# A block-Strassen feed-forward on one Trainium2 core: the block sums of its weights, made by VectorE or by accumulating loads

## The chip, the core and the metric

One core of a Trainium2 chip runs the whole step. Its engines are TensorE (PE, matrix products; PEld is its weight load), VectorE (DVE), ScalarE (ACT), GpSimd (POOL) and SyncE (SP, which here only issues loads and stores). Each engine runs its own instructions strictly in their written order and waits at an instruction until what it reads or overwrites is ready. The metric is the device time of one execution in microseconds (us). Before the change it was 1875.71 us, the median of three runs (1874.99 to 1875.91).

## The reference, cut to what matters

The program is one inference step of a two-layer decoder trunk for 576 token columns (a prompt of 512 and eight samples of eight). Each layer has a mixer (recurrent in the first layer, a state-space scan in the second), a feed-forward part and a gated embedding part, each behind an RMS norm:

```
def _swiglu(x, w1, w3, w2):
    return (jax.nn.silu(x @ w1) * (x @ w3)) @ w2
...
        x = x + mix
        x = x + _swiglu(_rmsnorm(x, W['g_ffn'][i]), W['ffn_w1'][i], W['ffn_w3'][i], W['ffn_w2'][i])
        x = x + _ple(x, p[i], W['ple_up'][i], W['ple_gate'][i], W['g_ple'][i])
```

`w1` and `w3` are 1024 x 2816 and `w2` is 2816 x 1024, all float32. The change is within `x @ w1` and `x @ w3`, of both layers.

## The kernel before

**Arithmetic.** Every float32 operand is kept as two fp32r tiles, a rounded high part and the rest (`whi`, `wlo` for weights, L171 to L176: ScalarE copies into `whi`, then VectorE, in some places GpSimd, subtracts into `wlo`). A product is three matmuls: high with high, high with low, low with high. Activations lie feature by token, 128 features to a tile; the 576 columns are two halves of 288.

**The up products.** `ffn` (L1057 on) does `x @ w1` and `x @ w3` by Strassen's scheme in the variant of Winograd: the weights of a pair of 128-column groups, called a block here and `p` in the code, are four quarter tiles `w13[p, 0..3]` of 128 x 1024 float32 (512 KB), and a block takes seven products of 24 matmuls (L1112 to L1121) instead of eight. In the order of TensorE they are: quarter 1 (`mmy`), the sum `u` of quarters 2, 3 and 0 (`mmx`), the sum of quarters 2 and 3 (`mmz`), the sum of quarters 2 and 0 (`mmx`), quarter 0 of the next block (`head`, L1128), quarter 3 (`mmx`), and `u` with quarter 1 added (`mmz`). There are 11 blocks in a layer, done in three parts of 4, 4 and 3 blocks (`PARTS`); behind each part the eight down products with `w2` follow (L1174 to L1175, matmuls of L210).

**The sums before.** SP loads the four quarters a second time into tiles `a2`, `a3`, `a0`, `a1` (L1154, by way of L1110), one buffer each. VectorE makes the sums: `a22 += a21` (L1157; both by their Strassen names), `u = a22 + a11` (L1158), `a21 += a11` (L1163), and after the second product has split `u`, `u += a12` (L1173). Each sum is then split into `whi` and `wlo` by L174 and L175. Plain quarters pass through `raw` tiles with two buffers (L166 to L169).

**What sets the order.** The code is written in the order of the data; a scheduler that works on a timed model of the engines sets the order of each engine's instructions when the program is built, and places waits on semaphores. A load is issued by SP when its tile's last readers are done, and SP's loads too stand in one order.

**Ahead of each feed-forward.** In the first layer the last instructions of the mixer are its output products: TensorE's `mm` (L193) into two PSUM buffers, VectorE's residual add (L361), and GpSimd's `wlo` for them (L175). The products of the embedding part (`ple_up`, L193 with `xah`) follow, and fill TensorE while the norm is made: squares (L349, L350), their sum over features (`ssq`, L233), the inverse root on VectorE (L236 to L246), the broadcast `rbc` on TensorE (L252) and its copy `rb` (L255). Then VectorE makes the scaled input (L1092) and the operands of the seven products. In the second layer the residual adds are done by GpSimd (L359) from a scaled copy that VectorE makes (L358).

Of the kernel before, what the change touches and what calls it, by code (L numbers as in the profile page):

```python
# [12 lines left out]
F = mybir.dt.float32  # L13
# [4 lines left out]
OP = mybir.AluOpType  # L18

P = 128  # L20
D = 1024
KD = D // P
# [58 lines left out]
def trunk(ctx, tc, a, stop=None):  # L81
    nc = tc.nc
    V, S, G, PE = nc.vector, nc.scalar, nc.gpsimd, nc.tensor

    cp = ctx.enter_context(tc.tile_pool(name="const", bufs=1))
    wp = ctx.enter_context(tc.tile_pool(name="weights", bufs=2))
# [44 lines left out]
    def tmp(tag, bufs=2, w=T, dt=F):  # L131
        return tp.tile([P, w], dt, tag=tag, name=tag, bufs=bufs)

    def bank(name="s", tag="s"):
        return pq.tile([P, 512], F, tag=tag, name=name)
# [20 lines left out]
    def split_to(dst, src, scale=None):  # L156
        hi, lo = dst
        if scale is None:
            S.activation(hi, src, AF.Copy)
            V.tensor_tensor(lo, src, hi.bitcast(F), op=OP.subtract)  # L160
        else:
            S.activation(hi, src, AF.Copy, scale=scale)
            V.scalar_tensor_tensor(lo, src, scale, hi.bitcast(F), op0=OP.mult, op1=OP.subtract)  # L163
        return hi, lo
# [6 lines left out]
    def wsplit(raw, kt, pool, bufs, w=1024, eng=V):  # L171
        hi = pool.tile([P, w], R, tag="whi", name="whi", bufs=bufs)[:, :kt * P]
        lo = pool.tile([P, w], R, tag="wlo", name="wlo", bufs=bufs)[:, :kt * P]
        S.activation(hi, raw, AF.Copy)  # L174
        eng.tensor_tensor(lo, raw, hi.bitcast(F), op=OP.subtract)  # L175
        return hi, lo  # L176
# [6 lines left out]
    def wload(ap, kt, eng=V):  # L183
        return wsplit(wraw(ap, kt), kt, wp, 2, eng=eng)
# [874 lines left out]
    def ffn(i, ha):  # L1059
        w13, w2 = a["w13"][i], a["w2"][i]  # L1060
        with tc.tile_pool(name=f"ffn{i}", bufs=1) as hp:

            def hq():
                return [hp.tile([P, 4, T], R, tag="h" + t_, name="h" + t_, bufs=2) for t_ in "hl"]
# [12 lines left out]
            def operand(n, src, scale=None):  # L1077
                out = []
                for ks, hi, lo in keep(n):
                    split_to((hi, lo), src[:, ks[0]:ks[-1] + 1], scale)  # L1080
                    out += [(hi[:, j], lo[:, j]) for j in range(len(ks))]
                return out
# [18 lines left out]
            b1 = operand(3, d1)  # L1101
            b3 = operand(4, d3)
# [1 line left out]
            b4 = operand(5, d4)  # L1104
            b22 = operand(6, xg1[:, :, HF:])

            def wsum(tag, src=None):
                t = hp.tile([P, 1024], F, tag=tag, name=tag, bufs=1)
                if src is not None:
                    nc.sync.dma_start(t, src)  # L1110
                return t

            def prod(outs, wts, b, first):
                wh, wl = wts
                for n in range(2):
                    for k in range(4):
                        o = slice(n * SEQ + k * P, n * SEQ + (k + 1) * P)
                        h, l = b[k]
                        for t_, (w, v) in enumerate(((wh, h), (wh, l), (wl, h))):
                            PE.matmul(outs[n], w[:, o], v, start=(first and k == 0 and t_ == 0), stop=(k == 3 and t_ == 2),  # L1120
                                      skip_group_check=not first)  # L1121

            def copied(ps, tag):
                t = v2(tmp(tag, 2))
                S.activation(t, ps[:, :, :HF], AF.Copy)  # L1125
                return t

            def head(p):  # L1128
                ps = pm.tile([P, 2, 512], F, tag="mm", name="mmx")
                prod([ps[:, n, :HF] for n in range(2)], wload(w13[p, 0], KD), b11, True)  # L1130
                return ps, copied(ps, "t1")

            def block(s, outs, dst, sign):
                for n in range(2):
                    V.tensor_tensor(s[:, n], s[:, n], outs[n], op=OP.add)
                S.activation(s[:, 0], s[:, 0], AF.Silu, scale=sign)
                if sign > 0:
                    V.tensor_tensor(dst, s[:, 0], s[:, 1], op=OP.mult)
                else:
                    V.scalar_tensor_tensor(dst, s[:, 1], sign, s[:, 0], op0=OP.mult, op1=OP.mult)  # L1140

            for p0, p1 in PARTS:
                hs = []
                for p in range(p0, p1):
                    if p == p0:
                        ps, s1 = head(p)
                    if (p - p0) % 2 == 0:
                        hh, hl = hq()
                    o = 2 * ((p - p0) % 2)
                    xo = [ps[:, n, :HF] for n in range(2)]  # L1150
                    ys = [bank("mmy")[:, :HF] for _ in range(2)]
                    prod(ys, wload(w13[p, 1], KD), b21, True)
                    f1, f2 = tmp("rb", 2), tmp("t2", 2)
                    block(s1, ys, f1[:, :HF], 1.0)  # L1154
                    a21, a22, a11, a12 = (wsum(f"a{n}", w13[p, n]) for n in (2, 3, 0, 1))
                    u = wsum("u")
                    V.tensor_tensor(a22, a22, a21, op=OP.add)  # L1157
                    V.tensor_tensor(u, a22, a11, op=OP.add)  # L1158
                    prod(xo, wsplit(u, KD, wp, 2), b2, False)
                    s2 = copied(ps, "t2")  # L1160
                    zs = [bank("mmz", "o")[:, :HF] for _ in range(2)]
                    prod(zs, wsplit(a22, KD, wp, 2), b1, True)
                    V.tensor_tensor(a21, a21, a11, op=OP.add)  # L1163
                    prod(xo, wsplit(a21, KD, wp, 2), b3, False)
                    s3 = copied(ps, "t1")
                    block(s3, zs, f2[:, HF:], -1.0)
                    if p + 1 < p1:
                        nxt = head(p + 1)
                    prod(xo, wload(w13[p, 3], KD), b4, False)
                    S.activation(f2[:, :HF], xo[0], AF.Silu, scale=-1.0)  # L1170
                    V.scalar_tensor_tensor(f2[:, :HF], xo[1], -1.0, f2[:, :HF], op0=OP.mult, op1=OP.mult)
                    split_to((hh[:, o + 1], hl[:, o + 1]), f2)
                    V.tensor_tensor(u, u, a12, op=OP.add)  # L1173
                    prod(zs, wsplit(u, KD, wp, 2), b22, False)  # L1174
                    block(s2, zs, f1[:, HF:], 1.0)  # L1175
                    split_to((hh[:, o], hl[:, o]), f1)
                    hs += [(hh[:, o + 1], hl[:, o + 1]), (hh[:, o], hl[:, o])]
                    ps, s1 = nxt
                for m in range(KD):
                    add_out(m, gemm(w2[m][:, 2 * p0 * P:2 * p1 * P], hs, False))  # L1180
# [278 lines left out]
```

## Time and profile before

| What | Before |
|---|---|
| median of the runs | 1875.71 us |
| the profiled execution's own time | 1873.93 us |
| its span | 1872.2 us |
| TensorE busy | 1748.0 us, 93% |
| VectorE busy | 1343.1 us, 72% |
| ScalarE busy | 811.7 us, 43% |
| GpSimd busy | 415.1 us, 22% |
| second loads of the quarters | 88 of 512 KB |
| bytes moved | 193.74 MB, mean 103 GB/s |

The span runs from the first to the last instruction of the profiled execution; the execution's own time holds what lies around it as well. Engines run side by side, so that their busy times don't add up; for this kernel the question at each place is on what TensorE waits. In the views below, a wait stands as "[idle before <- what ended it]" behind an instruction. A busy TensorE shows in the count of its matmuls as well: at full clock some 77 of them start in 10 us. TensorE's granted clock is given as a share of full speed.

### The profile page before, as it was taken

Reading aid. Unit: us, or ns where it says so; the run is one execution under the profiler, and the core shown is the slowest. Engines: PE = TensorE matmul, PEld = TensorE weight load, DVE = VectorE, ACT = ScalarE, POOL = GpSimd, SP = SyncE. Lnnn points to the kernel's source line nnn. Section 1 sums busy time; section 2 is a strip of 40 time slices with the busy share of each in tenths; the row PEclk is TensorE's granted clock in tenths of the full one; section 3 lists DMA queues with packets and bytes.
Section 4 is the critical chain, followed back from the end, with each engine's and each line's share of the span. In section 5 each row is a group of like instructions: output and inputs, shape, how many; then the busy total and the mean of one; then the engine's idle time right before and its main releaser. Section 6 shows DMA issues by size and latency. Waiting matters only on the chain. (4 is left out here: it accounts for less than half of the span.)

```text
span 1872.2 us, 32247 instructions
## 1 busy us (share of the span) xinstructions
PE 1748.0 (93%) x13134; PEld 1693.6 (90%) x13134; DVE 1343.1 (72%) x2256; ACT 811.7 (43%) x1341; POOL 415.1 (22%) x393
## 2 busy tenths in 40 slices
PE   7899989899999999989998999998959999999994
PEld 7789979899999999989987999998959999999994
DVE  6877784886377375588996897988587637737556
ACT  6654442554254143444553444535444325415332
POOL 2433343000000000033445537455510000000002
PEclk9999999899999999989998999999979999999997
DMA  5111113244244242312231322223315424424221
GB/s 191 57 62 66 68 49 130 83 160 139 91 162 154 87 147 71 118 41 72 103 111 68 109 104 85 96 100 108 118 52 167 133 86 168 147 91 144 71 80 51
DMA packets 63124, 193.74 MB, mean 103 GB/s; under 512 B 7040, under 2 KB 12800, under 8 KB 62976
## 3 DMA queue, kind: packets, MB, share of 16 engines
q1 hardware_dynamic: 62400, 191.10, 29.8%
q8 instruction: 103, 1.69, 0.4%
q10 hardware_dynamic: 576, 0.59, 0.1%
q14 instruction: 45, 0.37, 0.1%
HBM read 177.10 MB, written 14.56 MB: 102 GB/s over the span
## 5 line engine op out<-in xcount | busy, mean ns | idle before, releaser
L174 ACT ACTIVATE whi<-wraw 128x1024 fp32r<-128x1024 f32 (+2 forms) x213 | 221.5, 1040 | 392.6 <-PE mm L210 175.3
L175 DVE TENSOR_TENSOR wlo<-wraw,whi 128x1024 fp32r<-128x1024 f32 (+1 forms) x187 | 230.4, 1232 | 73.8 <-ACT whi L174 73.0
L1220 POOL TENSOR_TENSOR ev<-ev,rb 128x288 f32<-128x288 f32 x18 | 18.1, 1034 | 952.7 <-ACT rb L255 952.7
L1120 PE MATMUL mmx<-bh,whi 128*128 128x288 f32 x704 | 211.9, 301 | 14.8 <-ACT t L1125 9.3
L1120 PE MATMUL mmx<-bh,wlo 128*128 128x288 f32 x704 | 210.6, 299 | 4.8 <-DVE wlo L175 4.7
L1120 PE MATMUL mmx<-bl,whi 128*128 128x288 f32 x704 | 210.6, 299 | 2.9 <-DVE bl L163 2.9
L193 PE MATMUL mm<-xah,whi 128*128 128x288 f32 x632 | 191.4, 303 | 3.7 <-DVE hz L264 1.7
L193 PE MATMUL mm<-xal,whi 128*128 128x288 f32 x632 | 190.2, 301 | 0.0
L193 PE MATMUL mm<-xah,wlo 128*128 128x288 f32 x632 | 189.4, 300 | 0.0
L361 DVE TENSOR_TENSOR x<-mm,x 128x288 f32<-128x288 f32 x128 | 52.4, 451 | 169.1 <-PE mm L210 159.1
L193 PE MATMUL mm<-xch,whi 128*128 128x288 f32 x536 | 161.4, 301 | 2.9 <-DVE x L361 2.9
L193 PE MATMUL mm<-xch,wlo 128*128 128x288 f32 x536 | 160.8, 300 | 0.0
L193 PE MATMUL mm<-xcl,whi 128*128 128x288 f32 x536 | 160.7, 300 | 0.0
L210 PE MATMUL mm<-hl,whi 128*128 128x288 f32 x704 | 152.0, 296 | 0.0
L210 PE MATMUL mm<-hh,whi 128*128 128x288 f32 x704 | 151.7, 296 | 0.0
L210 PE MATMUL mm<-hh,wlo 128*128 128x288 f32 x704 | 151.3, 296 | 0.0
L1120 PEld LDWEIGHTS mmx<-bh,whi 128*128 128x128 f32 x704 | 134.5, 191 | 16.9 <-ACT t L1125 10.7
L1120 PEld LDWEIGHTS mmx<-bh,wlo 128*128 128x128 f32 x704 | 135.2, 192 | 6.6 <-DVE wlo L175 6.5
L1120 PEld LDWEIGHTS mmx<-bl,whi 128*128 128x128 f32 x704 | 134.9, 192 | 3.1 <-DVE bl L163 3.1
L193 PEld LDWEIGHTS mm<-xah,whi 128*128 128x128 f32 x632 | 120.0, 190 | 7.8 <-ACT lt L497 2.1
L193 PEld LDWEIGHTS mm<-xal,whi 128*128 128x128 f32 x632 | 120.2, 190 | 2.4 <-issue 1.8
L193 PEld LDWEIGHTS mm<-xah,wlo 128*128 128x128 f32 x632 | 120.1, 190 | 1.6 <-issue 0.9
(495 smaller groups left out, 4927.4 us busy)
## 6 DMA issues: line engine op xcount, KB each, us to landing
wraw<-w SPq DMA_DIRECT2D x98, 512.0 KB, 3.4
a<-w SPq DMA_DIRECT2D x88, 512.0 KB, 3.3
wraw<-w_sin SPq DMA_DIRECT2D x40, 512.0 KB, 3.3
wraw<-w_ein SPq DMA_DIRECT2D x22, 512.0 KB, 3.3
wraw<-wg SPq DMA_DIRECT2D x16, 512.0 KB, 3.2
s<-ss SPq DMA_DIRECT2D x16, 512.0 KB, 3.5
sss<-s SPq DMA_DIRECT2D x16, 512.0 KB, 2.8
wraw<-w_sout SPq DMA_DIRECT2D x16, 512.0 KB, 3.6
```

Source lines behind the costliest of these rows:

```text
L174: S.activation(hi, raw, AF.Copy)
L175: eng.tensor_tensor(lo, raw, hi.bitcast(F), op=OP.subtract)
L193: PE.matmul(ps, w[:, cols], v, start=(k == 0 and i == 0), stop=(k == n - 1 and i == 2))
L210: PE.matmul(ps[:, s, :HF], w[:, j * P:(j + 1) * P], m[:, half(s)], start=(k == 0 and i == 0), stop=(k == n - 1 and i == 2))
L361: V.tensor_tensor(xh, src, xh, op=OP.add)
L1120: PE.matmul(outs[n], w[:, o], v, start=(first and k == 0 and t_ == 0), stop=(k == 3 and t_ == 2), skip_group_check=not first)
L1220: eng.tensor_tensor(v, v, r[:, half(s)], op=OP.mult)
```

## The change

SP now loads one quarter into each of three tiles, `u`, `sa` and `sb`, which have two buffers each, and GpSimd issues loads of the further quarters that add onto the tile as they land (`accum_op`): two onto `u` ahead of its first use, one onto `sa`, one onto `sb`, and one more onto `u` when its first split has been made. The four additions on VectorE are gone.

```diff
-            def wsum(tag, src=None):
-                t = hp.tile([P, 1024], F, tag=tag, name=tag, bufs=1)
-                if src is not None:
-                    nc.sync.dma_start(t, src)
+            def wsum(tag, p, *blocks):
+                t = hp.tile([P, 1024], F, tag=tag, name=tag, bufs=2)
+                nc.sync.dma_start(t, w13[p, blocks[0]])
+                for n in blocks[1:]:
+                    add_block(t, p, n)
                 return t
+
+            def add_block(t, p, n):
+                nc.gpsimd.dma_start(t, w13[p, n], accum_op=OP.add)
...
-                    a21, a22, a11, a12 = (wsum(f"a{n}", w13[p, n]) for n in (2, 3, 0, 1))
-                    u = wsum("u")
-                    V.tensor_tensor(a22, a22, a21, op=OP.add)
-                    V.tensor_tensor(u, a22, a11, op=OP.add)
+                    u, s1_, s3_ = wsum("u", p, 2, 3, 0), wsum("sa", p, 2, 3), wsum("sb", p, 0, 2)
                     prod(xo, wsplit(u, KD, wp, 2), b2, False)
...
-                    prod(zs, wsplit(a22, KD, wp, 2), b1, True)
-                    V.tensor_tensor(a21, a21, a11, op=OP.add)
-                    prod(xo, wsplit(a21, KD, wp, 2), b3, False)
+                    prod(zs, wsplit(s1_, KD, wp, 2), b1, True)
+                    prod(xo, wsplit(s3_, KD, wp, 2), b3, False)
...
-                    V.tensor_tensor(u, u, a12, op=OP.add)
+                    add_block(u, p, 1)
                     prod(zs, wsplit(u, KD, wp, 2), b22, False)
```

The order of the instructions changes in these places. On VectorE, within a block (the first layer's second one), the rows before were these; `wlo<-a` are splits of sums:

```order
L175 TENSOR_TENSOR wlo<-a_3935,whi 128x1024
L175 TENSOR_TENSOR wlo<-wraw,whi 128x1024
L1157 TENSOR_TENSOR a_4185<-a_4185,a_4183 128x1024
L1163 TENSOR_TENSOR a_4183<-a_4183,a_4187 128x1024
L175 TENSOR_TENSOR wlo<-wraw,whi 128x1024
L1135 TENSOR_TENSOR t_4035<-t_4035,mmz 128x288 x2
L175 TENSOR_TENSOR wlo<-u,whi 128x1024
```

and they are now, with `sb` in the place of the tile `a`:

```order
L175 TENSOR_TENSOR wlo<-sb,whi 128x1024
L175 TENSOR_TENSOR wlo<-wraw,whi 128x1024 x2
L1139 TENSOR_TENSOR t_4031<-t_4031,mmz 128x288 x2
L1144 SCALAR_TENSOR_TENSOR t_3928<-t_4031 128x288
L175 TENSOR_TENSOR wlo<-u,whi 128x1024
```

The two additions for the next block no longer stand ahead of the split of a plain quarter. On GpSimd, at the end of the first layer's mixer, the difference is this (`-` before, `+` now; `wlo` belongs to the mixer's output products):

```order
-L175 TENSOR_TENSOR wlo<-wraw,whi 128x1024 x3
+L175 TENSOR_TENSOR wlo<-wraw,whi 128x1024 x2
+L1115 DMA u<-w 128x1024
+L1115 DMA sa<-w 128x1024
+L1115 DMA sb<-w 128x1024
+L175 TENSOR_TENSOR wlo<-wraw,whi 128x1024
```

Three accumulating loads of the first block now stand ahead of the last `wlo`, and each waits for the plain load beneath it. On GpSimd at the end of the second layer's mixer the rows before were these, `x_75`, `x_76` and so on being the eight tiles of the residual:

```order
L175 TENSOR_TENSOR wlo<-wraw,whi 128x1024
L359 TENSOR_TENSOR x_75<-x_75,t_14369 128x288
L359 TENSOR_TENSOR x_75<-x_75,t_14372 128x288
L175 TENSOR_TENSOR wlo<-wraw,whi 128x1024
L359 TENSOR_TENSOR x_76<-x_76,t_14400 128x288
L359 TENSOR_TENSOR x_76<-x_76,t_14403 128x288
L359 TENSOR_TENSOR x_77<-x_77,t_14437 128x288
L359 TENSOR_TENSOR x_77<-x_77,t_14440 128x288
```

and they are now:

```order
L1115 DMA u<-w 128x1024
L1115 DMA sa<-w 128x1024
L1115 DMA sb<-w 128x1024
L359 TENSOR_TENSOR x_75<-x_75,t_14347 128x288
L359 TENSOR_TENSOR x_75<-x_75,t_14350 128x288
L1115 DMA u<-w 128x1024
L1115 DMA sa<-w 128x1024
L359 TENSOR_TENSOR x_76<-x_76,t_14378 128x288
L359 TENSOR_TENSOR x_76<-x_76,t_14381 128x288
L175 TENSOR_TENSOR wlo<-wraw,whi 128x1024
L1115 DMA sb<-w 128x1024
```

Two more loads of `u` follow among the adds of the tiles behind: eight in all, three ahead of the first add and five between the adds. On TensorE the order of the matmuls within the feed-forward is the same as before. Ahead of the first layer's, the broadcast of the norm (`rbc`) stood before among matmuls of `ple_up` like this (`mm_3422` and `mm_3437` are two of its products, of 12 matmuls each):

```order
L193 MATMUL mm_3422<-xah_3346,wlo_3419 128x288
L252 MATMUL rbc_3531<-cst_73,ry_3516 128x128 x4
L252 MATMUL rbc_3537<-cst_73,ry_3516 128x64
L193 MATMUL mm_3437<-xah_3333,whi_3418 128x288
L193 MATMUL mm_3437<-xal_3334,whi_3418 128x288
```

and stands now:

```order
L193 MATMUL mm_3437<-xal_3347,whi_3418 128x288
L193 MATMUL mm_3437<-xah_3346,wlo_3419 128x288
L252 MATMUL rbc_3531<-cst_73,ry_3516 128x128 x4
L252 MATMUL rbc_3537<-cst_73,ry_3516 128x64
L193 MATMUL mm_3452<-xah_3333,whi_3418 128x288
```

Twelve matmuls that came behind the broadcast now come ahead of it.

## Rows read from the trace of the kernel before

**Rows 1.** Stretches (up, down): busy PE, PEld, DVE, ACT, POOL; clock, DMA share, GB/s

```profile
388.00:454.00 66.00, 63.88 (x478) 63.41 (x478) 53.14 (x68) 32.52 (x47) 0.00 (x0) 1.00 0.46 160
600.00:657.00 57.00, 57.00 (x430) 57.00 (x429) 21.51 (x32) 12.23 (x15) 0.00 (x0) 1.00 0.29 93
```

**Rows 2.** PE's waits, 375 to 750 and 1400 to 1750: total us, times, longest

```profile
PE mmx L1120 <- ACT t L1125: 4.7, 3, 1.6
PE mmx L1120 <- DVE wlo L175: 1.1, 2, 0.6
...
PE mmx L1120 <- DVE wlo L175: 3.4, 3, 1.6
```

**Rows 3.** Timeline of DVE and PE, 1449 to 1460 us: start, us, what

```profile
1450.73 1.23 DVE L175 TENSOR_TENSOR wlo<-wraw,whi 128x1024 fp32r<-128x1024 f32 x1 [1.92 <-ACT whi L174]
1454.33 1.22 DVE L1157 TENSOR_TENSOR a<-a,a 128x1024 f32<-128x1024 f32 x1 [2.37 <-DMA a<-w]
1455.59 1.23 DVE L1163 TENSOR_TENSOR a<-a,a 128x1024 f32<-128x1024 f32 x1
1456.73 1.22 DVE L175 TENSOR_TENSOR wlo<-wraw,whi 128x1024 fp32r<-128x1024 f32 x1
...
1458.01 0.40 PE L1120 MATMUL mmx<-bh,wlo 128*128 128x288 f32 x1 [1.61 <-DVE wlo L175]
```

**Rows 4.** Two of the four sums over the run: ns minimum/median/maximum

```profile
L1157 DVE TENSOR_TENSOR a<-a,a x22: 1224/1226/3197, 323.9 to 1716.6; 128x1024 f32<-128x1024 f32 x22
...
L1173 DVE TENSOR_TENSOR u<-u,a x22: 1214/1218/1220, 371.2 to 1729.9; 128x1024 f32<-128x1024 f32 x22
```

**Rows 5.** Timeline of DVE, PE and POOL at the first layer's mixer end

```profile
323.59 2.39 POOL L175 TENSOR_TENSOR wlo<-wraw,whi 128x1024 fp32r<-128x1024 f32 x1 [4.60 <-ACT whi L174]
...
323.87 3.20 DVE L1157 TENSOR_TENSOR a<-a,a 128x1024 f32<-128x1024 f32 x1 [0.91 <-DMA a<-w]
...
327.85 0.40 PE L193 MATMUL mm<-xch,whi 128*128 128x288 f32 x1 [2.17 <-DVE x L361]
331.61 0.37 PE L193 MATMUL mm<-xch,whi 128*128 128x288 f32 x1 [0.32 <-DVE x L361]
```

**Rows 6.** Timeline of PE and DVE from the first layer's norm on

```profile
347.05 1.22 PE L252 MATMUL rbc<-cst,ry 128*128 128x128 f32 x10
...
348.89 5.92 DVE L1092 SCALAR_TENSOR_TENSOR hh<-x,par,rb 128x576 f32<-128x576 f32 x8 [1.03 <-ACT rb L255]
```

**Rows 7.** Second layer's mixer end: POOL's waits 1338 to 1372; timelines

```profile
POOL x L359 <- DVE t L358: 11.8, 5, 6.7
...
1343.94 1.56 POOL L359 TENSOR_TENSOR x<-x,t 128x288 f32<-128x288 f32 x2 [6.71 <-DVE t L358]
...
1366.67 2.52 POOL L359 TENSOR_TENSOR x<-x,t 128x288 f32<-128x288 f32 x2 [1.95 <-DVE t L358]
...
1339.18 1.23 DVE L1157 TENSOR_TENSOR a<-a,a 128x1024 f32<-128x1024 f32 x1
...
1343.41 0.81 DVE L358 TENSOR_TENSOR t<-mm,rb 128x288 f32<-128x288 f32 x2
...
1370.84 2.26 PE L233 MATMUL ssq<-cst,acc 128*128 128x1 f32 x10 [7.17 <-DVE acc L350]
```

**Rows 8.** SP's issue of the second loads: ns minimum/median/maximum

```profile
L1110 SPq DMA_DIRECT2D a<-w x88: 327/328/433, 316.1 to 1713.3; - x88
```

**Rows 9.** Loads issued 380 to 450, then 310 to 330: us to landing; slices

```profile
a<-w SPq DMA_DIRECT2D x12, 512.0 KB, 3.3
...
a<-w SPq DMA_DIRECT2D x4, 512.0 KB, 7.6
...
GB/s 33 188 406 385 37 0 106 401 401 139 0 0 101 217 373 400 236 205 279 197 238 238 320 320 369 377 401 426 418 434 361 246 164 98 188 377 352 49 57 33
```

**Rows 10.** Timelines of DVE and ACT: the two splits of one block's u

```profile
391.47 1.23 DVE L175 TENSOR_TENSOR wlo<-u,whi 128x1024 fp32r<-128x1024 f32 x1
...
406.22 1.06 ACT L174 ACTIVATE whi<-u 128x1024 fp32r<-128x1024 f32 x1 [1.60 <-PE mmx L1120]
```

## The prediction

> **What bounds the kernel now.** I read the busy times by stretch first, because the change lives in the up products alone. In a stretch of three whole blocks [rows 1] TensorE is busy for 63.88 of 66 us and VectorE for 53.14, at full clock; GpSimd does nothing. TensorE bounds these stretches, and VectorE's share of 81% costs only where TensorE has to wait for it. So the next view is what TensorE waits for there [rows 2]. In nearly all of the two feed-forward parts it waits for ScalarE's copies, three times 1.6 us in each layer (4.7 us and 4.7 us; the same row for both), which the change doesn't touch, and for VectorE's `wlo`: 1.1 us in the first layer and 3.4 us in the second, five waits in 22 blocks. The timeline of the longest [rows 3] shows how they come about. VectorE ends a split at about 1452, then stands 2.37 us at L1157, whose quarter hasn't landed; L1163 follows, and only then the split of the plain quarter that TensorE needs: it waits 1.61 us. A late load thus stops VectorE's whole queue. Last I read the two places ahead of the feed-forward parts [rows 5 to 7], where VectorE's sums and now GpSimd's loads stand among work that TensorE waits for.
>
> **What goes.** 88 additions on VectorE: four kinds, 22 each, of some 1.22 us [rows 4], together 88 x 1.22 = 107 us. Nearly all lie beside TensorE's matmuls and are worth nothing. On the path are:
>
> - The `wlo` waits, 1.1 + 3.4 = 4.5 us. Without L1157, no load can stop VectorE there, and the split comes right behind ScalarE's copy. I take all 4.5. The bound below is 2.5, if the waits only shrink: then ScalarE's spacing of its copies holds part of them.
> - First layer, end of the mixer: a sum took 3.20 us beside a GpSimd `wlo` of 2.39 us that ran at the same time [rows 5], against 1.22 us undisturbed; TensorE then waited 2.17 and 0.32 us for the residual adds behind it, 2.5 us. But the new order puts twelve matmuls ahead of the broadcast `rbc`. A matmul takes 63.88 us / 478 = 0.13 us [rows 1], so that is 1.6 us. `rbc` to L1092 is the path here: `rbc` runs at 347.05, L1092 starts at 348.89 and paces the start of the feed-forward [rows 6]. So 2.5 - 1.6 = 0.9 us is left of it.
> - Second layer, end of the mixer: the sums from 1339.18 on hold the first scaled copy until 1343.41 [rows 7]; without them it starts up to 4.2 us earlier, of which I count two sums, 2.4 us, as the norm must be broadcast first.
>
> **What comes.** 22 x 3 = 66 loads by SP for 88, and 22 x 5 = 110 accumulating loads that GpSimd issues.
>
> *The issue.* No row before shows a load that GpSimd issues. Below, SP's issue of the same shape takes 0.33 us [rows 8]; above, GpSimd's own pass over such a tile takes 2.39 us [rows 5]. Both rows are near in their own way, the first in kind of work, the second in engine, so I take the middle, 1.4 us. In the feed-forward itself GpSimd is empty, and five issues are 7 us of a block of 22 us: hidden. Ahead of the second layer's they are not. Three issues fall into a stretch of 6.71 us in which GpSimd waited for its first add [rows 7], 4.2 us: hidden, if the plain loads beneath have landed. Five stand between the adds: 5 x 1.4 = 7.0 us, against waits of 11.8 - 6.7 = 5.1 us among the later adds [rows 7]. So GpSimd ends its adds 1.9 us later, and the last add is on the path: TensorE waited 7.17 us for the norm's sum that hangs on it. Against the 2.4 us gained above, I book this place as 0; its bounds are 2.4 gained, if an issue costs 0.33 us, and 5 x 2.39 - 5.1 - 2.4 = 4.4 lost.
>
> Ahead of the first layer's part, three issues stand before the last `wlo` of the mixer, which started at 323.59 and was needed by about 331.6 [rows 5]. The loads under it took 7.6 us to land [rows 9], from 316.1 [rows 8], thus until about 324; the third one comes a load's transfer of 1.25 us (worked out below) behind. Then 1.4 us, then the `wlo` of 2.39 us: done at 329.0, when TensorE, without its 2.5 us of waits, wants it at 329.1. So nothing is lost at 1.4 us; at 2.39 us two or three microseconds are. Range of this place: 2.5 gained to 2 lost.
>
> *The transfer.* A block moved seven loads of 512 KB (0.524 MB) in 22 us; now it moves eleven, five of which read or write the tile as well. In slices with loads back to back the engines moved 401 to 434 GB/s [rows 9], so a plain load costs them 0.524 / 0.42 = 1.25 us. If an accumulating load costs r plain ones, a block wants (6 + 5r) x 1.25 us: 13.8 us at r = 1, 20.0 at r = 2, 26.3 at r = 3. No row sets the bound above. I take 1.5, near the plain load, the only row there is: 16.9 us, hidden in the 22.
>
> The row [rows 9] knows plain loads alone. The Trainium skill (Collectives: The Full Stack, "The bandwidth ceiling: the fold count and why AG ≠ RS ≠ AR") speaks against the change: an add in the DMA engines needs two source reads through one read ring, and there halved the throughput, 32.35 against 62.28 GB/s. By that r is about 2, and 20.0 of 22 us are in use; no run before shows it. The sum stays as it is, but the margin is 10%, and a later fall of it is likelier than by r = 1.
>
> *The waits.* SP's loads wait for buffers as before, with two of each. GpSimd's queue has one new danger: the third load onto `u` must come between the two splits of `u`. The first ends at 391.47 + 1.23 = 392.7, the second starts at 406.22 [rows 10]: 13.5 us for its issue, transfer and landing, where a plain load takes 3.3 us [rows 9]. Behind it in the queue stand the loads for the next blocks, which are wanted half a block later or more. Cover enough for a landing of 5 to 8 us.
>
> **The sum.** 4.5 + 0.9 + 0 = 5.4 us less. The profiled execution took 1873.93 us (its span of 1872.2 and 1.7 around it), so 1868.5; the median of the runs, 1875.71, lies 1.8 above it, so I predict 1870.3. With the bounds: at best 4.5 + 2.5 + 2.4 = 9.4 less, 1866; at worst 2.5 - 2 - 4.4, 3.9 more, 1879.6.
>
> **Rivals.**
>
> *A, slower: the accumulating loads are too dear for the engines.* Place: every block. It decides from (22 / 1.25 - 6) / 5 = 2.3 plain loads each. At r = 3.3 a block wants 28.1 us, 6.1 too many: 24.5 in a part of four blocks, 18.4 in one of three. The down products between (57 us at a share of 0.29 [rows 1]) let four of a block's five sums run ahead, 4 x 3.3 x 1.25 = 16.5 us. What stays is 4 x 8.0 + 2 x 1.9 = 36 us: 1875.7 + 36 - 5 = 1906. At r = 4 it is over 100 us. Milder and in the same mechanism: the third load onto `u` lands after 13.5 us, and every block waits; a microsecond each gives 1892. For it: nothing in the trace bounds r, and the margin at 2 is small. Against: the engines' mean share is 0.46 in the up stretches [rows 1].
>
> *B, no change: GpSimd's queue gives it back.* If an issue takes 2.39 us, the two mixer ends lose 2 + 4.4 = 6.4 us and the 4.5 are spent: 1875.7 + 1.9 = 1877.6. For it: GpSimd is the slowest engine for everything else; against: SP's issue takes a seventh of that [rows 8].
>
> *C, no change: another wait stands behind the one removed.* TensorE's waits for `wlo` end with ScalarE's copies: if these are half of it, and the moved `rbc` eats the first layer's gain, 2.3 us remain: 1873.4. For it: 1.92 us of VectorE's idle time ahead of a split is put down to ScalarE [rows 3]. Against: that split wasn't waited for.
>
> **Chances.** Forecast 0.48, A 0.27, B 0.13, C 0.12. What a measurement can tell here from no change is 0.2%, 3.7 us. Of the forecast some 0.04 is below that. So faster 0.44, the same 0.04 + 0.13 + 0.12 = 0.29, slower 0.27. The range goes from 1865 to 1900: it takes in the forecast, B and C, and of A the milder half; what is left out is some 0.15 above and 0.02 below. The forecast's own range is 1866 to 1880, B and C being within it.
>
> **What would show it.** Right: VectorE's busy time in the run down by some 107 us and no wait of TensorE on `wlo` in the blocks but at their start; the six waits for ScalarE of 1.6 us unchanged; GpSimd's issues below 2 us; a DMA share in the up stretches between 0.6 and 0.9. The first layer's L1092 starts about 1 us earlier than 348.89, the second layer's sum of squares within 2 us of 1370.84. Wrong: TensorE waits on the split of `u`, `sa` or `sb`, which in turn waits on a load; then A holds, and the landing time of these loads gives r. If TensorE's waits ahead of the feed-forward parts grow while the blocks run clean, it is B.

## The result, and the profile after

The changed kernel takes 1906.11 us in the median of four runs (1901.38 to 1907.46) against 1875.35 us before (1874.83 to 1875.91): the ratio is 1.0159 with a 95% interval of 1.0141 to 1.0178. The forecast was 1870.3 with a range of 1865 to 1900: the time moved the other way, and it lies 6 us past the top of the range.

I read the page first. These are its busy line and its lines on the DMA queues (queue, packets, MB, and the time that their packets took as a share of 16 engines over the span of 1903.7 us):

```profile
PE 1760.1 (92%) x13134; PEld 1706.1 (90%) x13134; DVE 1249.4 (66%) x2168; ACT 814.0 (43%) x1341; POOL 510.2 (27%) x503
...
q1 hardware_dynamic: 59232, 179.56, 27.0%
q0 software_dynamic: 15840, 57.68, 16.3%
```

VectorE fell from 1343.1 to 1249.4 us: 93.7 us, of the 107 that 88 times 1.22 us make, since rows that follow each other at once overlap by about 0.1 us (in [rows 3], 1455.59 + 1.23 against 1456.73). GpSimd's own queue, q0, now carries the 110 added loads. Its share gives their price: 16.3% of 1903.7 us are 310 us, over 110 loads 2.82 us of all engines for each. The plain loads of q1 take 27.0% for 179.56 MB, which is 1.50 us for 512 KB.

The two stretches of [rows 1], now three blocks and a down part (columns as there):

```profile
388.00:454.00 66.00, 66.00 (x499) 66.00 (x497) 41.38 (x57) 33.97 (x48) 11.13 (x13) 1.00 0.91 231
600.00:657.00 57.00, 50.36 (x361) 50.12 (x360) 20.14 (x29) 12.57 (x16) 4.35 (x5) 0.94 0.62 157
```

The blocks run clean: TensorE is busy for all of the 66 us, at a DMA share of 0.91 where it was 0.46. The loss is in the second stretch, which here takes in the end of a part of the feed-forward. The waits of [rows 2], for 375 to 750 and, since all is later now, 1400 to 1800:

```profile
PE mmx L1124 <- ACT t L1129: 14.7, 3, 6.6
...
PE mmx L1124 <- ACT t L1129: 11.4, 3, 5.0
...
PE mmx L1124 <- DVE wlo L175: 0.9, 2, 0.7
```

The waits for `wlo` are nearly gone (1.1 + 3.4 us before, 0.9 now). But the waits for ScalarE's copy, which were 1.6 us at each of three part ends in a layer, are now up to 6.6 us at the first two. The timeline of ScalarE, VectorE and GpSimd at the first layer's first part end shows why (L1115 is an added load, L174 and L175 the two halves of a split, L1129 the copy that TensorE waits for):

```profile
437.85 0.33 SPq L1109 DMA_DIRECT2D u<-w  x1
...
441.97 1.04 ACT L174 ACTIVATE whi<-u 128x1024 fp32r<-128x1024 f32 x1
443.04 1.23 DVE L175 TENSOR_TENSOR wlo<-u,whi 128x1024 fp32r<-128x1024 f32 x1 [0.19 <-ACT whi L174]
...
447.05 1.76 POOL L1115 DMA_DIRECT2D u<-w  x2 [10.05 <-DVE wlo L175]
...
455.49 0.86 POOL L1115 DMA_DIRECT2D u<-w  x1 [6.68 <-DMA u<-w]
...
459.13 1.06 ACT L174 ACTIVATE whi<-u 128x1024 fp32r<-128x1024 f32 x1 [7.07 <-DMA u<-w]
460.09 0.63 ACT L1129 ACTIVATE t<-mmx 128x576 f32<-128x576 f32 x1
```

The first split of `u` was done at 443.04 + 1.23 = 444.27, and the third load onto `u` could have been issued then. GpSimd issued a pair only from 447.05 on. By the order of the code and the semaphores, the first of the two is the next block's first load onto its own `u`, which waits until the plain load under it has landed; that one left SP at 437.85. (The row names `wlo` as the releaser, but that was long done.) The third load is the second of the pair, issued at about 447.95, 3.7 us late. Then it took until 459.13, 11.2 us, and ScalarE stood for 7.07 us at the split with the copy that TensorE needs behind it in its queue. The next block's second load followed at 455.49, when the first had landed.

The stall costs more than its length. The same place in slices of 10 us (PE busy with its matmuls, PEld, DVE, ACT, POOL; the sixth column is the granted clock):

```profile
440.00:450.00 10.00, 10.00 (x77) 10.00 (x76) 8.45 (x13) 5.55 (x9) 1.76 (x2) 1.00 0.95 262
450.00:460.00 10.00, 4.29 (x33) 4.05 (x31) 1.41 (x2) 1.93 (x2) 2.62 (x3) 0.83 1.02 252
460.00:470.00 10.00, 9.22 (x49) 9.23 (x50) 4.37 (x7) 3.10 (x6) 0.66 (x1) 0.66 0.75 175
```

TensorE stood still for more than half of the second slice, and the granted clock fell to 0.83 and 0.66 of full speed, a mix of the levels 2.4 and 1.2 GHz; 49 matmuls started in the third slice instead of 77. At the other three places with such a stall, too, a slice of 10 us shows 0.66 (from 610, 1500 and 1645 us).

To add it up I compared the start of each run of matmuls with the same one before; the difference is called the lag below. The profiled execution is 31.5 us longer in its span; the last of these starts lies 31.2 us behind. From front to end this is made of: 3.9 us in the first mixer, whose instructions are unchanged (see the last section); 3.3 us at the first layer's start; 6.0 us won within the blocks of both layers; 7.6 and 7.9 us lost at the first layer's first two part ends, none at the third; 2.6 us won between the two feed-forward parts, where nothing was changed (ten of the twelve runs below won 1.0 to 2.3 there, the one whose sums VectorE makes 1.5); 6.0 us lost at the second layer's start; 6.0 and 5.1 us at its first two part ends. So 26.6 us are part ends and 9.3 us layer starts.

The third part end of a layer tells something by itself. No further block follows there, so that no load of a next block stands ahead of the third load onto `u`. In the first layer it was issued at 722.36, landed after 5.4 us, and cost nothing:

```profile
722.36 0.86 POOL L1115 DMA_DIRECT2D u<-w  x1 [17.06 <-DVE wlo L175]
```

At the layer starts, loads are late too. ScalarE at the end of the first and of the second layer's mixer:

```profile
338.17 1.06 ACT L174 ACTIVATE whi<-wraw 128x1024 fp32r<-128x1024 f32 x1 [7.00 <-DMA wraw<-wup]
...
1374.07 1.06 ACT L174 ACTIVATE whi<-wraw 128x1024 fp32r<-128x1024 f32 x1 [6.55 <-DMA wraw<-w_sout]
```

The weights of the last mixer products and of the embedding part stand in SP's queue behind six loads for the first two blocks, and GpSimd's added loads go at the same time.

### The profile page after: what moved, and what is told of

Its sections match the earlier page's. It is cut to its first block, busy times and chain, and to the rows that moved or that the text cites. A ratio compares the mean times of both kernels' runs of the same rounds, so it can differ in the third digit from the quotient of the medians.

```text
span 1903.7 us, 32376 instructions
## 1 busy us (share of the span) xinstructions
PE 1760.1 (92%) x13134; PEld 1706.1 (90%) x13134; DVE 1249.4 (66%) x2168; ACT 814.0 (43%) x1341; POOL 510.2 (27%) x503
## 3 DMA queue, kind: packets, MB, share of 16 engines
q1 hardware_dynamic: 59232, 179.56, 27.0%
q0 software_dynamic: 15840, 57.68, 16.3%
## 5 line engine op out<-in xcount | busy, mean ns | idle before, releaser
L174 ACT ACTIVATE whi<-wraw 128x1024 fp32r<-128x1024 f32 (+2 forms) x213 | 221.5, 1040 | 421.7 <-PE mm L210 175.4
L175 DVE TENSOR_TENSOR wlo<-wraw,whi 128x1024 fp32r<-128x1024 f32 (+1 forms) x187 | 230.3, 1232 | 152.8 <-ACT whi L174 152.0
L1124 PE MATMUL mmx<-bh,whi 128*128 128x288 f32 x704 | 216.1, 307 | 33.5 <-ACT t L1129 26.1
L1124 PE MATMUL mmx<-bl,whi 128*128 128x288 f32 x704 | 215.0, 305 | 2.6 <-DVE bl L163 2.2
L1115 POOL DMA_DIRECT2D u<-w x66 | 58.6, 938 | 573.7 <-DVE wlo L175 320.9
L1124 PEld LDWEIGHTS mmx<-bh,whi 128*128 128x128 f32 x704 | 138.5, 197 | 35.5 <-ACT t L1129 27.7
L1124 PEld LDWEIGHTS mmx<-bl,whi 128*128 128x128 f32 x704 | 138.9, 197 | 3.4 <-DVE bl L163 2.7
L1124 PEld LDWEIGHTS mmx<-bh,wlo 128*128 128x128 f32 x704 | 139.1, 198 | 1.7 <-DVE wlo L175 1.7
L193 PEld LDWEIGHTS mm<-xah,whi 128*128 128x128 f32 x632 | 120.8, 191 | 16.6 <-ACT t L349 5.0
```

The lines of the kernel that those rows point to most:

```text
L193: PE.matmul(ps, w[:, cols], v, start=(k == 0 and i == 0), stop=(k == n - 1 and i == 2))
L1115: nc.gpsimd.dma_start(t, w13[p, n], accum_op=OP.add)
```

## The experiments

T1 says that the adding loads cost too much: the engines are full, and all loads land late. T2 says that the order of GpSimd's queue does it. T3 says that it is the number of loads alone. A theory S, on the layer starts, comes in with its runs. Four kernels at a time ran on one chip with the kernel before, whose medians were 1874.49, 1875.75 and 1874.71 us; each ratio is to the runs of before beside it.

### Loads that don't add

```diff
-                nc.gpsimd.dma_start(t, w13[p, n], accum_op=OP.add)
+                nc.gpsimd.dma_start(t, w13[p, n])
```

> As the changed kernel, but the five loads of a block that GpSimd issues overwrite the tile instead of adding onto it; so the sums are left out. Same loads, bytes, issues, order and waits. Theory T1 (an accumulating load costs the DMA engines about 1.9 plain loads, so that they are saturated and every load lands late): a plain load costs 1.5 us of all engines, 11 of them 16.5 us of a block's 22; these loads land in 4 to 5 us instead of 8.4, the part ends lose 2 us or less each instead of 6.5, the layer starts go back, and the time is 1870 to 1880 us. Theory T2 (the order of GpSimd's queue: the third load onto u stands behind the next block's first load onto u, which waits for its plain load): the queueing stays, so each part end still loses 3 us or more and the time is 1885 to 1895. Theory T3 (eleven loads in place of seven, whatever their kind): no change, 1903 to 1908.

Measured: 1873.47 us, ratio 0.9992 (0.9980 to 1.0004). Its line on GpSimd's queue:

```profile
q0 software_dynamic: 15840, 57.68, 9.1%
```

The transfer of the third load at the first part end (DMA view of 441.0 to 441.5; count, size, us from issue to landing):

```profile
u<-w POOLq DMA_DIRECT2D x1, 512.0 KB, 4.2
```

T3 falls for the part ends, and for the time as a whole: the same loads in the same order give the time of before when they don't add. But the layer starts did not go back, as T1 had expected. By its trace this kernel loses 3 to 4 us at the first one and 2.2 at the second, where the changed kernel lost 3.3 and 6.0, and its blocks win that back; ScalarE waits there 6.71 us for `wup` and 4.40 us for `w_sout`, and nothing adds. A load costs 9.1% of 1871.7 us / 110 = 1.55 us, so that an adding one costs 2.82 / 1.55 = 1.8 plain ones. T2 had three microseconds lost at each part end; none was. With loads that land sooner (the plain one under `u` in 4.7 us, 7.6 in the changed kernel) GpSimd doesn't stand at all: it issued the third load at 441.06, 0.3 us after the split. So at the part ends the order alone is harmless as well.

### The third load first

```diff
+                with after_all(last_add[0] if tag == "u" else None):
+                    for n in blocks[1:]:
+                        add_block(t, p, n)
...
+                    last_add[0] = add_block(u, p, 1)
```

> As the changed kernel, but the first two added loads onto the next block's u are held behind the third one onto this block's u in GpSimd's queue. T2 (queue order): the third load is issued at once when u's first split is done, about 3 us earlier at the part ends; the four part ends lose 3 us instead of 6.5 or nothing, time 1880 to 1892. T1 (saturated engines): the landing takes the same 8 to 11 us after the issue, and the next u is completed later, so that what is won at the part ends comes back as waits in the blocks: 1895 to 1908. T3: as T1.

Measured: 1877.98 us, ratio 1.0022 (1.0010 to 1.0033): 27 of the 31 us are gone with the order alone, while all five loads still add. The timeline of GpSimd and ScalarE at the first part end:

```profile
442.10 0.86 POOL L1118 DMA_DIRECT2D u<-w  x1 [7.86 <-DVE wlo L175]
444.18 0.86 POOL L1118 DMA_DIRECT2D u<-w  x1 [1.22 <-DMA u<-w]
...
452.12 1.06 ACT L174 ACTIVATE whi<-u 128x1024 fp32r<-128x1024 f32 x1 [2.14 <-PE mmx L1127]
```

The slice of 440 to 450 us, whose second last column is the share of the DMA engines:

```profile
440.00:450.00 10.00, 10.00 (x77) 10.00 (x77) 6.47 (x9) 5.50 (x8) 1.72 (x2) 1.00 1.06 264
```

And the transfer of the third load (DMA view of 442.0 to 442.9):

```profile
u<-w POOLq DMA_DIRECT2D x1, 512.0 KB, 6.8
```

The time is better than T2's 1880 to 1892, and far from T1's 1895 to 1908. The third load goes out at 442.10, when the split is done at 441.80, and lands after 6.8 us; ScalarE waits for TensorE, not for a load. The window is 452.12 - 441.80 = 10.3 us. The engines are as full as in the changed kernel (share 1.06, and 16.6% of the span in q0), and no block waits. T1 in the form that full engines alone cost time falls too. For the loss at the part ends it takes both: loads that add, and the order.

### The third load alone adds

```diff
-                nc.gpsimd.dma_start(t, w13[p, n], accum_op=OP.add)
+                nc.gpsimd.dma_start(t, w13[p, n], **({"accum_op": OP.add} if n == 1 else {}))
```

> As the changed kernel in all orders and waits, but of GpSimd's five loads of a block the third one onto u alone adds onto the tile; the other four overwrite it, so that the sums are left out but for quarter 1. A block wants 10 x 1.55 + 2.83 = 18.3 us of the engines. If the price of the third load itself closes the window: part ends lose 2 to 4 us each, 1880 to 1888. If it is the crowd of the other four (the engines are full when it comes, and the next block's plain load that GpSimd waits for lands late): 1870 to 1877.

Measured: 1873.04 us, ratio 0.9989 (0.9978 to 1.0000). GpSimd issues the next `u`'s first load and this `u`'s third one as a pair again:

```profile
438.61 1.44 POOL L1115 DMA_DIRECT2D u<-w  x2 [9.44 <-DVE wlo L175]
```

The transfers of the first (DMA view of 438.5 to 438.9) and the second of the pair (439.2 to 439.9):

```profile
u<-w POOLq DMA_DIRECT2D x1, 512.0 KB, 4.0
...
u<-w POOLq DMA_DIRECT2D x1, 512.0 KB, 6.9
```

So the third load takes 4.2 us when nothing adds, 6.9 us when it alone adds, 6.8 us when all add and it goes first, and 11.2 us when all add and it stands behind the next `u`'s first load. Its own addition doesn't close the window. Nor do the others lengthen its landing where they only run beside it, as they do with the third load first. What differs in the changed kernel is the adding load directly ahead; the 4.4 us are put down to it by this comparison, as no run has these two loads alone adding. With the third load first it is the next `u`'s first load, now the second of the two, that takes 9.8 us. The crowd has its part in the 3.7 us before: the plain load that GpSimd stands at lands late because the engines are full. 3.7 + 11.2 = 14.9 us don't go into 10.3; 6.8 and 6.9 do.

### The last addition on VectorE

```diff
+                    a12 = wsum("a1", p, 1)
...
-                    add_block(u, p, 1)
+                    V.tensor_tensor(u, u, a12, op=OP.add)
```

> As the changed kernel, but the last quarter is added to u by VectorE from a tile that SP loads ahead (sb and that tile have one buffer each); GpSimd issues four accumulating loads for a block in place of five. The window between the two splits of u then holds no load. T1 and T2 alike lose the 26 us at the part ends: 1878 to 1884. What tells them apart is what stays: T1 (a block wants 7 x 1.5 + 4 x 2.8 = 22 us of the engines, still all of it) leaves the landing times at 8 us and waits on sa, sb or u in the blocks, 1884 to 1895; T2 leaves nothing but the layer starts, 1875 to 1881.

Measured: 1877.64 us, ratio 1.0014 (0.9999 to 1.0028). The waits at the part ends are back at 1.6 us. Both theories had expected that; it confirms the place. The time itself is in T2's 1875 to 1881, below T1's 1884: four adding loads of a block still land after 7 to 9 us (medians of 6.8, 8.3 and 9.0), and the blocks don't pay for it. What is left are waits of 2.1 us for `wlo` in the second layer and the layer starts, 2.8 us each.

### One buffer, and one buffer with three for u

```diff
-                t = hp.tile([P, 1024], F, tag=tag, name=tag, bufs=2)
+                t = hp.tile([P, 1024], F, tag=tag, name=tag, bufs=2 if tag == "u" else 1)
```

The second kernel has 3 in place of 2 there.

> As the changed kernel, with one buffer each for sa and sb, and nothing held: in GpSimd's queue the third load onto u stands behind the next block's first load onto u, as in the changed kernel. If the order decides, the part ends lose some 6 us each, 24 more than the 1867.7 us of the run with one buffer and the third load first: 1886 to 1896. If the buffers decide (fewer loads that crowd the engines at once, landings shorter): 1867 to 1876.

> As the run with one buffer each for sa and sb, and three buffers for u: the third load onto u still stands behind the next block's first one in GpSimd's queue, but that one's plain load no longer waits for a tile, so that it has landed long before. T2 (the third load is late because GpSimd stands at a load whose plain load hasn't landed): no loss at the part ends, 1866 to 1874. If the landing time of the third load itself is enough (T1): 1885 to 1896.

Measured: 1899.34 us, ratio 1.0131 (1.0109 to 1.0154), and 1899.92 us, ratio 1.0129 (1.0105 to 1.0152). The first says that the order decides, at 3 us more than I had put as the most. The second didn't do what it was for: the scheduler used the third buffer to issue one block further ahead, so that GpSimd again stood at a load whose plain load hadn't landed. GpSimd and ScalarE at the first part end:

```profile
441.56 1.75 POOL L1115 DMA_DIRECT2D u<-w  x2 [8.92 <-DMA u<-w]
...
453.63 1.06 ACT L174 ACTIVATE whi<-u 128x1024 fp32r<-128x1024 f32 x1 [6.70 <-DMA u<-w]
```

Here the row names the load itself. The wait at a part end came out as in the changed kernel; whether a plain load that has landed early would have helped wasn't tested by it.

These two kernels also show the queue's order at work in a second place. At the second layer's start they lose 5.8 and 5.3 us, as much as the changed kernel, though four and five plain loads and not six stand ahead of the mixer's weights. With one buffer, ScalarE doesn't wait for those weights there; GpSimd stands at a load onto the second block's `u`, which waits for the one before it onto the same tile, and the residual adds stand behind:

```profile
1370.26 0.89 POOL L1115 DMA_DIRECT2D u<-w  x1 [6.54 <-DMA u<-w]
1370.87 1.11 POOL L359 TENSOR_TENSOR x<-x,t 128x288 f32<-128x288 f32 x1
```

### The layer starts

The first block of each layer by VectorE, in the changed kernel and with the third load first:

```diff
+                    if p:
+                        u, s1_, s3_ = wsum("u", p, 2, 3, 0), wsum("sa", p, 2, 3), wsum("sb", p, 0, 2)
+                    else:
+                        s3_, s1_, a11, a12 = wsum("sa", p, 2), wsum("sb", p, 3), wsum("sa", p, 0), wsum("sb", p, 1)
+                        u = hp.tile([P, 1024], F, tag="u", name="u", bufs=2)
+                        V.tensor_tensor(s1_, s1_, s3_, op=OP.add)
+                        V.tensor_tensor(u, s1_, a11, op=OP.add)
```

> As the changed kernel, but the first block of each layer makes its sums on VectorE from four plain loads; GpSimd's order behind it is as in the changed kernel. Theory S (at a layer's start the six loads of the first two blocks and the loads added to them delay the mixer's last weights, which costs 3 us in the first layer and 6 in the second beside the part ends): 1896 to 1902. Rival (the starts cost nothing of their own; the part ends are all of it): 1904 to 1908.

> Third load first in GpSimd's queue, as in the run before, and the first block of each layer made by VectorE. The run with the third load first alone lost 0.7 us at the first layer's start and 3.6 at the second's by its trace and took 1878.0 us. Theory S: these go, 1872 to 1875. Rival (the starts' loss comes from the new order of the other engines, not from the loads): 1877 to 1879.

Measured: 1899.45 us, ratio 1.0124 (1.0107 to 1.0142), and 1874.83 us, ratio 1.0006 (0.9993 to 1.0018). Both times are where theory S had them; the traces bear it out in the first layer alone. By them the first one gains 0.9 us at the first layer's start and loses 3.0 at the second's, where the changed kernel lost 3.3 and 6.0. The second one gains 0.8 and loses 4.0 us, more than the 3.6 of the run with the third load first; and each loses 2.0 more at the second layer's first block. That the second one's time is in S's range isn't shown to come from the layer starts, and may be luck: its profile is ahead of the one with the third load first by 4.4 us in the first mixer, which isn't changed, and 3 us behind it in the rest. At the second layer's start the loads come in time; VectorE's three sums stand ahead of the mixer's scaled copies again, one of them at a late load:

```profile
1337.73 1.23 DVE L1168 TENSOR_TENSOR u<-sb,sa 128x1024 f32<-128x1024 f32 x1 [1.26 <-DMA sa<-w]
1338.88 1.22 DVE L1174 TENSOR_TENSOR sa<-sa 128x1024 f32<-128x1024 f32 x1
1340.01 0.81 DVE L358 TENSOR_TENSOR t<-mm,rb 128x288 f32<-128x288 f32 x2
```

Then the third load first with one buffer each for `sa` and `sb`, so that four plain loads and not six stand ahead of the mixer's last weights:

```diff
+                t = hp.tile([P, 1024], F, tag=tag, name=tag, bufs=2 if tag == "u" else 1)
...
+                with after_all(last_add[0] if tag == "u" else None):
```

> Third load first in GpSimd's queue, and sa and sb with one buffer each (u keeps two), so that four plain loads stand ahead of the mixer's last weights in place of six, and three added loads in place of up to seven. Theory S: the second layer's start loses 1 to 2 us less, 1874 to 1877. T1 in its strong form (saturated engines need all the time that two buffers give): waits on sa and sb in the blocks, 1882 or more.

Measured: 1867.70 us, ratio 0.9959 (0.9943 to 0.9975), better than I expected and faster than both kernels. The timeline at the second layer's mixer end shows VectorE's first scaled copy (L358), which came at 1340.01 in the run before, GpSimd among its adds (L359), and ScalarE's split of the mixer's weights, which in the changed kernel waited 6.55 us for a load:

```profile
1337.09 0.82 DVE L358 TENSOR_TENSOR t<-mm,rb 128x288 f32<-128x288 f32 x2 [1.94 <-ACT rb L255]
...
1344.36 0.85 POOL L1118 DMA_DIRECT2D u<-w  x1
1345.49 2.33 POOL L359 TENSOR_TENSOR x<-x,t 128x288 f32<-128x288 f32 x3 [0.28 <-DVE t L358]
1346.16 1.06 ACT L174 ACTIVATE whi<-wraw 128x1024 fp32r<-128x1024 f32 x1 [3.40 <-PE mm L193]
```

One added load stands among the adds where the changed kernel had five. Against before, its trace gains 2.3 us at the first layer's start, loses 0.8 within that layer's part, and gains 1.0 us at the second's start and 2.4 within its part. Its engines are as full as in the changed kernel (q0 takes 16.8% of the span).

Two things thus make the layer starts. One is the number of plain loads ahead of other weights: the five kernels with six of them (the changed one, loads that don't add, the third load first, the third alone adding, the last addition on VectorE) lose 0.7 to 4.0 us at the first layer's start, the four with four of them gain 0.8 to 2.3. The other is GpSimd's order: at the second layer's start four plain loads lose 5.8 us when an added load waits among the adds, and gain 1.0 when the third load goes first. No run moved the mixer's weights ahead of the loads in SP's queue and changed nothing else.

### Fewer additions by load, and VectorE's sums with more buffers

`sa` and `sb` by one adding load each, `u` and its last addition by VectorE (two buffers for `sa`; in the second kernel one):

```diff
+                    s1_, a11, s3_, a12 = wsum("sa", p, 2, 3), wsum("a0", p, 0), wsum("sb", p, 0, 2), wsum("a1", p, 1)
+                    u = hp.tile([P, 1024], F, tag="u", name="u", bufs=1)
+                    V.tensor_tensor(u, s1_, a11, op=OP.add)
...
+                    V.tensor_tensor(u, u, a12, op=OP.add)
```

> sa and sb are each made by one accumulating load; u and its last addition are made by VectorE from sa and from two plain loads (two buffers for sa, one for the rest). A block has nine loads, 7 x 1.55 + 2 x 2.83 = 16.5 us of the engines, and none between the two splits of u. T1 and T2 alike: no loss at the part ends, landings near 5 us, time 1870 to 1875. If VectorE's two sums are still stopped by late loads, the waits for wlo of the kernel before (4.5 us) stay and it is 1875 to 1878.

> As the run in which sa and sb are made by one accumulating load each and u by VectorE, but with one buffer for sa as well. If fewer early loads at the layer starts help here as they did with the third load first: 1864 to 1869. If VectorE's sum u, which reads sa, now holds the next block's sa back: 1871 to 1878.

Measured: 1870.63 us, ratio 0.9964 (0.9951 to 0.9976), and 1869.68 us, ratio 0.9976 (0.9962 to 0.9990). The first is where it was expected, the second between its two ranges. The intervals overlap, so that the buffer of `sa` makes no difference that these runs can tell. Two adding loads in a block in place of five gain as much as the best one of five, as far as the intervals tell.

The last one is the kernel before, with a second buffer for the tile of quarter 2:

```diff
-                t = hp.tile([P, 1024], F, tag=tag, name=tag, bufs=1)
+                t = hp.tile([P, 1024], F, tag=tag, name=tag, bufs=2 if tag == "a2" else 1)
```

> The kernel before, with two buffers instead of one for the tile of quarter 2 (a2) alone; VectorE makes all the sums. If the late landing of that quarter is the whole cause of TensorE's waits for wlo (1.1 us in the first layer, 3.4 us in the second), as the forecast booked them, they go without any accumulating load: 1870 to 1872. If another wait stands behind them (ScalarE's copies, or another of the single tiles), 1874 to 1876.

Measured: 1875.61 us, ratio 1.0003 (0.9994 to 1.0013). TensorE's waits for `wlo` in the blocks are 1.3 and 1.2 us in place of 1.1 and 3.4; the gain of two microseconds is below what the runs can tell. In its trace the lag falls by about 1 us in the first layer's blocks and grows by 1.7 in the second's, where the changed kernel's fell by 6.0 in both together. This one buffer doesn't do what taking the sums from VectorE does; buffers for the other tiles weren't tried.

## Why the prediction was wrong, by its own steps

**What goes.** The step was right. I took 4.5 us for the waits for `wlo` [rows 2]; within the blocks the changed kernel gained 6.0 us by the comparison of starts. With the third load first the same 6 us show (the lag falls from 4.7 to 2.4 us in the first layer and from 4.0 to 0.3 in the second).

**The mixer ends.** I booked 0.9 us won and 0 and got 3.3 and 6.0 us lost. I looked at GpSimd's issues, VectorE's sums and the moved `rbc`, and left out which loads of others the new loads are moved ahead of. The second buffer let six loads stand ahead of the weights of the last mixer products and of `wup` in SP's queue, where before it had been four. The additions aren't needed for the loss in the first layer: without any, 3 to 4 us went there. In the second layer the order of GpSimd's queue is the other half: its added loads wait for one another, with the residual adds behind them. With four loads, and one addition among the adds, the places gain 2.3 and 1.0 us, near the forecast and better.

**The issue.** Taken at 1.4 us; the added load takes 0.86 us and the plain one of GpSimd 0.53. The error was on the safe side, so that rival B's price had nothing to stand on. Its place and its sign did: TensorE's waits ahead of the feed-forward parts grew while the blocks ran clean. What GpSimd can lose there is the wait for a load's landing (6.54 us at once in the run with one buffer each), which the step had set aside with "if the plain loads beneath have landed".

**The transfer.** Mis-sized twice. The plain load is 1.50 to 1.55 us of the engines, where I had 1.25 from the fastest slices [rows 9]: these were peaks, and the queue's share of the span would have given the mean. And an adding load is 1.8 plain ones, where I took 1.5. The Trainium skill (Collectives: The Full Stack, "The bandwidth ceiling: the fold count and why AG ≠ RS ≠ AR") has an add in the DMA engines halve the throughput of a collective, which makes about 2; the 1.8 of the loads here lies within a tenth of that. With the measured prices a block wants 6 x 1.50 + 5 x 2.82 = 23.1 us, more than its 22. Yet that isn't what cost the time: with the third load first the engines are as full, and the blocks don't wait, since loads run ahead beside the down products. Rival A had the right price in mind (it decides from 2.3 plain loads of 1.25 us, which is 2.9 us), but the wrong place. That its example, at 3.3 plain loads each, comes to 1906 us, the time measured, is chance: an adding load costs 1.8, and the loss isn't in every block.

**The waits.** This is the step that failed. I gave the third load onto `u` a window of 13.5 us from one block [rows 10], and wrote that behind it in the queue stand the loads for the next blocks. Both parts were wrong at one place. At a part's last block no `head` product stands between the two splits, and the window is 10.3 us. And ahead of the third load, not behind it, stands the next `u`'s first load, which GpSimd can't issue until its plain load has landed (3.7 us late at the first part end), and behind which, as it adds, the third load takes 11.2 us to land, where I had called 13.5 us cover enough for 5 to 8. The four part ends lost 26.6 us by it, which is most of the 31.2. The order of GpSimd's queue could have been read before; I read it for the two mixer ends and not here. The milder form of rival A (the third load lands too late) is what happened, four times at 5 to 8 us in place of each block at 1 us.

**The stall's price.** I counted waits alone. The waits at the four part ends grew by 10.0 us (14.7 - 4.7) and 6.7 us (11.4 - 4.7 over the whole second layer), 16.7 together; the part ends lost 26.6. The rest came behind them, where at each of the four a slice shows the granted clock at 0.66.

## What to carry to other kernels

When a load waits for something, list what stands ahead of it in its queue at the tightest place, the last block of a part, not the one in the middle: a queue that issues in order turns another load's wait into its own. An adding load is worth having where it isn't in a hurry: with the urgent one first and few loads ahead of the weights of other stages, the same five additions of a block gained 0.4%.

## What I had not expected of the hardware

- An adding load into a tile of 512 KB: 2.82 us of all DMA engines against 1.55 for a plain one on the same queue, 0.86 us against 0.53 to issue, and 6.8 to 6.9 us against 4.2 to land at a part end. Behind another adding load onto another tile it took 11.2 us.
- Full DMA engines needn't cost time: with the third load first their share is 1.00 from 400 to 450 us (a slice has 1.06, as packets' times are added up), and TensorE is busy for all of these 50 us.
- The first mixer, whose instructions are the same in all kernels here, took from 0.4 us less to 5.2 us more in the profiles of the other kernels than in that of the kernel before. Each kernel has one profile, so that it isn't known whether this goes with the execution or with the kernel. Its stretch of 125 to 135 us, in the kernel before, the changed kernel, and the run with the third load first and one buffer each (columns as in the slices above):

```profile
125.00:135.00 10.00, 8.28 (x63) 7.87 (x62) 9.07 (x17) 6.24 (x8) 5.15 (x4) 1.00 0.29 105
```

```profile
125.00:135.00 10.00, 8.28 (x42) 7.81 (x42) 9.06 (x17) 5.86 (x7) 5.21 (x4) 0.70 0.28 105
```

```profile
125.00:135.00 10.00, 8.39 (x64) 8.16 (x65) 9.08 (x17) 6.25 (x8) 4.85 (x3) 1.00 0.28 105
```

TensorE is busy for 8.3 us in each, after a wait for VectorE, and the granted clock is 1.00 in the first and the last and 0.70 in the changed kernel, where 42 matmuls start instead of 63 or 64. Of the 31.5 us between the two profiles 3.9 are this, and no step of the prediction is to be judged by them. Nor do differences of a few microseconds between the runs' profiles say much without that stretch. What decides on it stays open.
